# Running the first 128 tokens ahead of the second at the seams between stages of a decoder trunk

## The chip, the cores and the metric

The kernel runs on one core of one Trainium2 chip. The metric is the device time of one execution in microseconds, as the median over several runs. The engines are named as the profile names them: PE is TensorE's matrix multiplication and PEld its weight load, DVE is VectorE, ACT is ScalarE, POOL is GpSimd, SP is SyncE, whose queue issues the kernel's transfers. L12 is line 12 of the kernel that is spoken of; the changed kernel is longer, so the same helper has another line number there.

## The reference

Two layers of a decoder, 256 tokens of width 2048, in float32. Layer 0 mixes tokens with differential attention and an S5 state-space model side by side, layer 1 with RWKV-7. After each mixer comes a SwiGLU. Every mixer and every SwiGLU has an RMS norm ahead of it and one behind it.

```python
def _rwkv7_time_mix(x, mu, ...):
    x_prev = jnp.pad(x, ((0, 0), (1, 0), (0, 0)))[:, :-1]
    xx = x_prev - x
    xr, xw, xk, xv, xa, xg = (x + xx * mu[j] for j in range(6))
    r = xr @ w_r
    ...
    return out.astype(x.dtype) @ w_o

def _swiglu(h, w_gate, w_up, w_down):
    return (jax.nn.silu(h @ w_gate) * (h @ w_up)) @ w_down

for layer in range(DEPTH):
    gains = norm_gains[layer]
    h = _rmsnorm(x, gains[0])
    m = ...            # even: attention and S5, then w_out; odd: RWKV-7, then w_o
    x = x + _rmsnorm(m, gains[1])
    f = _swiglu(_rmsnorm(x, gains[2]), ffn_w_gate[layer], ffn_w_up[layer], ffn_w_down[layer])
    x = x + _rmsnorm(f, gains[3])
```

## The kernel before, in words

**Products.** The 256 tokens are two halves of 128, t = 0 and 1. A float32 product is made of three reduced-precision ones: each operand is split into a high and a low part, and the kernel adds high·high, high·low and low·high (`wmm`). The activations of one half are the stationary operand, 512 columns of the weights are moved through. One step of `wide` is one k (128 rows of the weights) for 512 columns, so three instructions of 128x512 for one half. Weights arrive in the order of use as chunks of eight 128x128 blocks (512 KB, two steps): a load on SP into `wr`, a cast on ACT into `wh`, a subtraction on DVE into `wl` (`chunk_load`, L321, L326, L327 before). Each of the three has three buffers, and the next load waits until a buffer is free.

**Seams.** A stage ends with its last group of 512 columns, for both halves. What follows needs the mean square of the whole row, so nothing of the next stage can start before. There are four such seams, named here after their place: A, from the output projection of layer 0 to the first SwiGLU's gate; B, from its down product to RWKV's `wr`; C, from RWKV's `wo` to the second SwiGLU's gate; D, from the last down product to the kernel's output. At each seam a half goes through an epilogue: `Out.add` adds a partial sum (A, C), sums the squares on ACT (L570) and multiplies by a gain (L571); L457 and L458 on DVE and L459 on POOL make the scale R. At A and C `stage` then adds the result to the residual (X, L1098, on DVE), multiplies by the next norm's gain row `gr` (L1099, on DVE for the first quad of four 128-column blocks, on POOL for the others), turns the blocks by "flips" on PE (L592, transposes into `pa`) and splits them into Z, high part on ACT (L403), low part on DVE (L409). At B the rows X are L1276, M = X·R1 is L1277, the flip goes into `pb`, ACT copies it to H (L1280), and `mix` makes x + xx·mu for 128 columns and all 256 tokens: L1249 on ACT, L1256 on DVE, the cast L403 into MX on ACT.

**Order.** A scheduler with priorities (`hi()`, XP) sets the order of each engine's queue when the kernel is built; while `strict` is set, PE keeps program order. An engine takes its queue in that order, also when a later instruction would be ready. At the end of a stage `late=LATE` makes the last four steps run for half 0 and then for half 1, and `warm` puts 20 products of no use (L309) behind the last one.

**Behind seam B.** `k_steps` runs seven 128-column products of `wr` (NR = 7) with the weights as the stationary operand and all 256 tokens moved through, k by k as the mixes of a quad come. Later in the layer `Q` blocks (QB) and state blocks (XI) go through DRAM (`dr`) and are loaded again by SP.

Of the kernel before, what the change touches and what calls it, by code (L numbers as in the profile page):

```python
# [18 lines left out]
P = 128  # L19
T = 256  # L20
# [33 lines left out]
LATE = 4  # L54
# [12 lines left out]
W1, W2, W3 = 20, 20, 20  # L67
# [144 lines left out]
class Prog:  # L212
# [104 lines left out]
    def chunk_load(self, c, raw=False, hp=None, pool=False):  # L317
        nc = self.nc
        with self.tc.high_priority(offset=HP if hp is None else hp):
            r = self.wp.tile([P, CB * P], F32, tag="wr", name=f"wr{c}")  # L320
            nc.sync.dma_start(r, self.d["wst"][c])  # L321
            if raw:
                return (r,)
            h = self.wp.tile([P, CB * P], F32R, tag="wh", name=f"wh{c}")
            l = self.wp.tile([P, CB * P], F32R, tag="wl", name=f"wl{c}")
            nc.scalar.copy(h, r)  # L326
            (nc.gpsimd if pool else nc.vector).tensor_tensor(l, r, h.bitcast(F32), op=ALU.subtract)  # L327
            return (h, l)

    def block(self, w, k, m, raw=False, pool=False):  # L330
# [4 lines left out]
        if b % CB == 0:  # L335
            c = b // CB
            self.wcur = self.ahead.pop(c, None) or self.chunk_load(c, raw, pool=pool)
# [4 lines left out]
    def blocks(self, w, k, m, n=4):  # L342
# [3 lines left out]
        for i in range(n):  # L346
            self.block(w, k, m + i)
# [173 lines left out]
    def wide(self, w, n, zH, zL, ks, pss, nb=4, late=0, hook=None, first=True, last=True):  # L521


        ks, held = list(ks), []
        o = [ps[:, :nb * P] for ps in pss]
        for a, k in enumerate(ks):
            self.lab(w)
            W = self.blocks(w, k, n, nb)
            f, e = first and a == 0, last and a == len(ks) - 1
            if a >= len(ks) - late:  # L530
                held.append((k, W, f, e))
                continue
            for t in range(2):
                self.wmm(o[t], zH[k], zL[k], W, t, f, e)
# [13 lines left out]
    class Out:  # L548


        def __init__(self, p, m, l, j, n=NW, xs=None):
            self.p, self.m, self.l, self.j, self.xs, self.i = p, m, l, j, xs, 0
            self.ss = [p.sp.tile([P, 3, n], F32, tag=f"ss{t}", name=p.nm("ss"), bufs=1) for t in range(2)]

        def add(self, pss, c, n=512, part=None, last=False):
            p, nc = self.p, self.p.nc
            v, gp = nc.vector, nc.gpsimd
            g, cs = p.gain_row(self.l, self.j, c, n), slice(c, c + n)
            for t in range(2):
                ss, m, ps = self.ss[t][:, :, self.i:self.i + 1], self.m[t][:, cs], pss[t][:, :n]  # L560
                junk = lambda: p.tmp("j", [P, n])
                xt = None
                if self.xs is not None:
                    xt = p.tmp("xt", [P, n])
                    nc.sync.dma_start(xt, self.xs[t][:, cs])
                with p.hi():
                    if part is not None:
                        v.tensor_tensor(m, ps, part[t][:, cs], op=ALU.add)
                        ps = m
                    nc.scalar.activation(junk(), ps, AF.Square, accum_out=ss[:, 0])  # L570
                    (gp if part is not None and not last else v).tensor_tensor(m, ps, g, op=ALU.mult)  # L571
                    if xt is not None:
                        (v if last else gp).tensor_tensor(xt, xt, m, op=ALU.mult)  # L573
                        nc.scalar.activation(junk(), m, AF.Square, accum_out=ss[:, 2])
                        nc.scalar.activation(junk(), xt, AF.Copy, scale=2.0, accum_out=ss[:, 1])
            self.i += 1
# [134 lines left out]
    def even(self):  # L711
        nc, v, gp = self.nc, self.nc.vector, self.nc.gpsimd
        with self.phase("ev"):
# [54 lines left out]
            def main():  # L768
# [41 lines left out]
                for n in range(NW):  # L810
                    pss = [self.pg(), self.pg()]
                    e = n == NW - 1
                    yield from self.wide("out", 4 * n, mH + gH, mL + gL, range(OH, 16), pss, late=LATE if e else 0)
                    out.add(pss, n * 512, part=part, last=e)
# [10 lines left out]
            self.warm(W1)  # L825
# [255 lines left out]
    def ffn(self, x, l, macc):  # L1081
# [4 lines left out]
        with self.phase(f"ffn{l}"):  # L1086
            sH, sL = ([self.slot("Z", 4, F32R) for _ in range(2)] for _ in range(2))
            zH, zL = ([s[k // 8][:, k % 8] for k in range(KD)] for s in (sH, sL))
            sx = [self.sp.tile([P, NW], F32, tag=f"sx{t}", name=self.nm("sx"), bufs=1) for t in range(2)]
# [19 lines left out]
            pss = [[self.pg(), self.pb()] for _ in range(3)]  # L1109
            grp = [(gw, 0), (uw, 0), (gw, 4)]  # L1110
            g = self.gain_row(l, 2, 0)
            for t in range(2):
                for k, n in ((0, 1), (1, 3)):
                    stage(t, k, n, g[:, k * P:(k + n) * P], v)
                if t == 0:
                    held = [self.blocks(gw, k, 0) for k in range(4)]
                for k in range(4):
                    self.lab(gw)
                    self.wmm(pss[0][t], zH[k], zL[k], held[k], t, k == 0, False)
            for q in range(4):  # L1120
# [681 lines left out]
```

## Time and profile before

| what | value |
|---|---|
| median of 3 runs | 2651.56 us (2647.16 to 2653.05) |
| the profiled execution | 2639.7 us, of which its span is 2637.9 us |
| PE busy | 2508.4 us (95%) |
| DVE busy | 1643.5 us (62%) |
| ACT busy | 1189.5 us (45%) |
| POOL busy | 444.8 us (17%) |
| mean granted clock | 0.972 |

The profiled execution is some 12 us below the median of the timed runs; sums made from its rows are set against its own time. A row of the timeline gives start, duration, engine, line, operation, output and inputs, and in brackets how long its engine was idle before it and what ended that. Busy shares are means over stages with different limits: what a seam costs is read at the seam.

### The profile page before, as it was taken

The page shows a single profiled execution, that of the slowest core. Times are in us where ns is not written, and L with a number is a line of the kernel's source. Part 1 is how long each engine was busy: PE and PEld are TensorE (multiplying, and loading weights), DVE is VectorE, ACT ScalarE, POOL GpSimd, SP SyncE. Part 2 cuts the span into 40 slices and gives each one's busy share as a digit, 9 for nine tenths or more (in the row PEclk, how much of TensorE's full clock was granted, in tenths as well). Part 3 has the DMA queues.
Part 4 walks back from the last instruction along what each step waited for, and adds up shares of the span by engine and source line. Part 5 has one row for each costly group of instructions (what it writes and reads, how often), then busy time and mean ns, then how long its engine had stood idle before and what let it go on. Part 6 is the DMA issues. An engine that isn't in the chain of part 4 may idle for free. (4 is left out here: it accounts for less than half of the span.)

```text
span 2637.9 us, 36715 instructions
## 1 busy us (share of the span) xinstructions
PE 2508.4 (95%) x13816; PEld 2097.0 (79%) x13816; DVE 1643.5 (62%) x2370; ACT 1189.5 (45%) x1752; POOL 444.8 (17%) x694
## 2 busy tenths in 40 slices
PE   7998899899999999997899898999799999999999
PEld 7775658688888888886899877788688888888887
DVE  7877876555555555445568987768655555554444
ACT  5332335444444444444666643343444444444443
POOL 4765731200000000000115540111300000000000
PEclk9998899999999999998999998999899999999999
DMA  6332335655555555665467677765655555555565
GB/s 217 116 108 66 103 112 194 210 186 186 190 190 191 186 192 189 208 224 199 144 200 241 201 215 206 193 192 184 205 187 187 191 191 190 190 187 192 196 195 192
DMA packets 222754, 484.51 MB, mean 184 GB/s; under 512 B 78832, under 2 KB 109808, under 8 KB 220784
## 3 DMA queue, kind: packets, MB, share of 16 engines
q1 hardware_dynamic: 222576, 482.17, 56.7%
q8 instruction: 108, 1.77, 0.3%
q14 instruction: 70, 0.57, 0.1%
HBM read 454.31 MB, written 27.79 MB: 183 GB/s over the span
## 5 line engine op out<-in xcount | busy, mean ns | idle before, releaser
L327 DVE TENSOR_TENSOR wl<-wr,wh 128x1024 fp32r<-128x1024 f32 x760 | 946.0, 1246 | 790.2 <-ACT wh L326 784.7
L326 ACT CAST wh<-wr 128x1024 fp32r<-128x1024 f32 x768 | 807.7, 1052 | 1039.7 <-PE pb L302 728.3
L302 PE MATMUL pg<-wh,Z 128*128 128x512 f32 x1664 | 636.8, 394 | 0.5 <-DVE Z L409 0.4
L302 PE MATMUL pb<-wh,Z 128*128 128x512 f32 x1408 | 547.2, 389 | 0.1
L302 PEld LDWEIGHTS pg<-wh,Z 128*128 128x128 f32 x1664 | 314.0, 189 | 71.2 <-issue 4.9
L302 PE MATMUL pg<-wl,Z 128*128 128x512 f32 x832 | 325.2, 391 | 0.0
L302 PEld LDWEIGHTS pb<-wh,Z 128*128 128x128 f32 x1408 | 264.2, 188 | 55.7 <-ACT Z L403 0.5
L302 PE MATMUL pb<-wl,Z 128*128 128x512 f32 x704 | 273.9, 389 | 0.0
L302 PE MATMUL pg<-wh,PP 128*128 128x512 f32 x576 | 223.3, 389 | 0.0
L302 PE MATMUL pb<-wh,PP 128*128 128x512 f32 x576 | 223.1, 389 | 0.0
L302 PE MATMUL pg<-MX,wh 128*128 128x256 f32 x896 | 175.3, 292 | 9.4 <-ACT MX L403 9.3
L302 PEld LDWEIGHTS pg<-wl,Z 128*128 128x128 f32 x832 | 157.4, 189 | 30.9
L302 PE MATMUL pg<-wh,MX 128*128 128x512 f32 x512 | 176.4, 409 | 0.3 <-ACT KR L1400 0.3
L302 PE MATMUL pg<-Z,wh 128*128 128x256 f32 x736 | 151.5, 306 | 16.2 <-ACT wh L326 10.5
L302 PEld LDWEIGHTS pb<-wl,Z 128*128 128x128 f32 x704 | 132.2, 188 | 27.5
L302 PEld LDWEIGHTS pg<-MX,wh 128*128 128x128 f32 x896 | 144.2, 196 | 10.7 <-ACT MX L403 9.9
L302 PEld LDWEIGHTS pg<-Z,wh 128*128 128x128 f32 x736 | 122.0, 205 | 36.4 <-issue 19.7
L302 PE MATMUL pg<-MX,wl 128*128 128x256 f32 x448 | 130.4, 294 | 3.9 <-DVE wl L327 3.9
L459 POOL TENSOR_TENSOR ts<-ts,mhalf 128x1 f32<-128x1 f32 x10 | 6.5, 653 | 752.4 <-DVE ts L458 752.4
L302 PEld LDWEIGHTS pg<-wh,PP 128*128 128x128 f32 x576 | 108.1, 188 | 22.5
L302 PEld LDWEIGHTS pb<-wh,PP 128*128 128x128 f32 x576 | 108.1, 188 | 22.5
L573 POOL TENSOR_TENSOR xt<-xt,M 128x512 f32<-128x512 f32 x6 | 7.8, 1300 | 666.0 <-DVE M L571 666.0
(402 smaller groups left out, 3758.2 us busy)
## 6 DMA issues: line engine op xcount, KB each, us to landing
wr<-wst SPq DMA_DIRECT2D x776, 512.0 KB, 3.4
dr<-H SPq DMA_DIRECT2D x16, 512.0 KB, 4.2
CH<-dr SPq DMA_DIRECT2D x16, 512.0 KB, 5.4
dr<-X SPq DMA_DIRECT2D x6, 1024.0 KB, 4.4
X<-dr SPq DMA_DIRECT2D x6, 1024.0 KB, 6.2
gr<-cr SPq DMA_DIRECT2D x16, 256.0 KB, 2.8
dr<-ak SPq DMA_DIRECT2D x16, 256.0 KB, 4.0
ln<-lnb SPq DMA_DIRECT2D x8, 512.0 KB, 5.0
```

Of the source, the lines that this page charges most:

```text
L302: self.pe(self.nc.tensor.matmul(out, lhsT, rhs, start=start, stop=stop))
L326: nc.scalar.copy(h, r)
L327: (nc.gpsimd if pool else nc.vector).tensor_tensor(l, r, h.bitcast(F32), op=ALU.subtract)
L459: self.nc.gpsimd.tensor_tensor(r, ms, self.mhalf[:, 0:1], op=ALU.pow)
L573: (v if last else gp).tensor_tensor(xt, xt, m, op=ALU.mult)
```

## The change

At each seam the last steps of the ending stage's last group and the first steps of the next are run for half 0 first, and for half 1 afterwards from weights that were kept. The kept chunks beyond the three buffers are put into memory that is not in use at that time ("homes": S, CH, Z, PA, PB, PC, MA). The numbers of steps are 8 (`LO0`) at A's end, 8 at C's, 12 (`LD`) at B's and D's, and 12 (`LO1`) of gate and 14 (`LW`) of `wr` for the stages that begin.

```diff
-LATE = 4
+LO0, LO1, LW, LD = 8, 12, 14, 12
-W1, W2, W3 = 20, 20, 20
...
+    def skew(self, w, zH, zL, steps, late, homes=(), pre=None, post=None):
+        held, homes = [], list(homes)
+        def piece(t, a, W):
+            k, n, o, f, e = steps[a]
+            if pre:
+                pre(t, a)
+            self.lab(w)
+            self.wmm(o[t], zH[k], zL[k], W, t, f, e)
+            if e and post:
+                post(t, n, o[t])
+        for a, (k, n, *_) in enumerate(steps):
+            keep = a >= len(steps) - late
+            home = homes.pop(0) if keep and homes and len(self.order) % CB == 0 else (None, False)
+            W = self.blocks(w, k, n, home=home[0], pool=home[1])
+            piece(0, a, W)
+            yield 2
+            if keep:
+                held.append((a, W))
+            else:
+                piece(1, a, W)
+                yield 2
+        for a, W in held:
+            piece(1, a, W)
+            yield 2
```

The gate's start, and one of the ends; `pre` puts the staging of a quad ahead of a step, `post` the epilogue of a half (`Out.half`, the old `Out.add` for one half) behind its last step. The 2 in `homes` sends that chunk's subtraction to POOL, in two pieces of 512 columns.

```diff
-            pss = [[self.pg(), self.pb()] for _ in range(3)]
-            grp = [(gw, 0), (uw, 0), (gw, 4)]
...
+            def pre(t, a):
+                if (t, a) == (0, 0):
+                    stage(0, 0, 1, gs[0][:, :P], v)
+                    stage(0, 1, 3, gs[0][:, P:], v)
+                    quad(0, 1)
+                elif (t, a) in ((0, 4), (0, 8)):
+                    quad(0, a // 4 + 1)
+                elif (t, a) == (0, 10):
+                    quad(1, 0, v)
+                elif (t, a) in ((1, 0), (1, 4), (1, 8)):
+                    quad(1, a // 4 + 1)
+            steps = [(k, 0, g, k == 0, False) for k in range(LO1)]
+            self.run(self.skew(gw, zH, zL, steps, LO1, [(("PC", 2), False), (("PC", 2), 2), (None, False), (None, 2), (pa, False),
+                                                        (pb, 2)], pre))
+            self.run(self.wide(gw, 0, zH, zL, range(LO1, KD), g, first=False))
+            self.run(self.wide(uw, 0, zH, zL, range(KD), u))
...
+            homes = [(("Z", 4), False)] * 3 if l else [(("PA", 4), False)] * 4
+            self.run(self.skew(dw, pH, pL, steps, LD, homes, post=lambda t, n, ps: out.half(t, NW - 1, ps, last=True)))
             x = self.load_x([a[:] for a in xs])
-            self.warm(W3 if l else W2)
```

The four gain rows are loaded together (`gs`, tiles e) with the priority XP; quad 1 of half 0 is turned ahead of the first gate product. In RWKV the first four `wr` columns become one group of 512 with the tokens as the stationary operand, whose result is turned back by eight flips (`turn`) and goes to DRAM in one tensor `r4`; columns 4 to 6 follow one after another. The mixes of a quad become 128x512 tiles: L1337 is ACT's scale of M, L1342 the copy to H, L1350 (L1347 for half 1) the product with mu on POOL, L1351 and L1352 DVE's product and sum, L418 the cast into MB on ACT. The mixes for the low-rank products, which are not part of `wr`, keep their form: L1300 and L1304 on ACT. The memory of the mixes (MX) is split in MA and MB, that of the SwiGLU's products (PP) in PA, PB and PC.

DVE's queue at seam A, from half 0's gain product on. Before (L571 gain product, L568 add, L1098 the rows X, L1099 the staging product; the two halves are M_4547 and M_4548):

```order
L571 TENSOR_TENSOR M_4547<-M_4547,t_4985 128x512
L457 TENSOR_REDUCE ts_5016<-ss_4549 128x1
L458 TENSOR_SCALAR ts_5017<-ts_5016 128x1
L327 TENSOR_TENSOR wl_5075<-wr_5072,wh_5074 128x1024
L568 TENSOR_TENSOR M_4548<-pg_4888,Z_3710 128x512
L1098 SCALAR_TENSOR_TENSOR X_5029<-M_4547,ts_5018,X_5029 128x128
...
L327 TENSOR_TENSOR wl_5134<-wr_5131,wh_5133 128x1024
L571 TENSOR_TENSOR M_4548<-M_4548,t_4985 128x512
...
L1098 SCALAR_TENSOR_TENSOR X_5030<-M_4548,ts_5024,X_5030 128x512 x3
L1099 TENSOR_TENSOR M_4547<-X_5029,gr_5048 128x128
```

And in the changed kernel (L613 gain product, L610 add, L1146 the rows X, L1147 the staging product):

```order
L613 TENSOR_TENSOR M_4547<-M_4547,t_4960 128x512
...
L1146 SCALAR_TENSOR_TENSOR X_5007<-M_4547,ts_4996,X_5007 128x512 x3
L342 TENSOR_TENSOR wl_5087<-wr_5084,wh_5086 128x1024
L610 TENSOR_TENSOR M_4548<-pg_4888,Z_3710 128x512
L613 TENSOR_TENSOR M_4548<-M_4548,t_4960 128x512
L472 TENSOR_REDUCE ts_5000<-ss_4550 128x1
L473 TENSOR_SCALAR ts_5001<-ts_5000 128x1
L1146 SCALAR_TENSOR_TENSOR X_5008<-M_4548,ts_5002,X_5008 128x512 x4
L342 TENSOR_TENSOR PC_5036<-wr_5034,PC_5036 128x1024
L1147 TENSOR_TENSOR M_4547<-X_5007,e_5015 128x128
L1147 TENSOR_TENSOR M_4547<-X_5007,e_5015 128x384
```

Half 0's X rows now stand ahead of half 1's add, but the first staging product of half 0 still stands behind half 1's X rows. POOL's queue at the same place, in the changed kernel (L474 is R's power; e_5017 is the gain row of quad 1):

```order
L474 TENSOR_TENSOR ts_5002<-ts_5001,mhalf 128x1
L342 TENSOR_TENSOR PC_5074<-wr_5072,PC_5074 128x512 x2
L342 TENSOR_TENSOR wl_5110<-wr_5107,wh_5109 128x512 x2
L1147 TENSOR_TENSOR M_4547<-X_5007,e_5017 128x512
L1147 TENSOR_TENSOR M_4548<-X_5008,e_5017 128x512
```

The two chunks' subtractions stand there between R and the first staging product; before, R was followed by L1099 at once. ACT's queue at seam B in the changed kernel, first at the first quads of half 0 and then at the last quads of half 1 (pb_10392 is the first quad's flip; MA_10869 to MA_10981 are the mixes for the low-rank products):

```order
L1337 ACTIVATE M_8639<-X_10333,ts_10342 128x512 x2
L612 ACTIVATE j_10325,ss_8642<-pb_9918 128x512
L1337 ACTIVATE M_8639<-X_10333,ts_10342 128x512
L616 ACTIVATE j_10329,ss_8642<-M_8640 128x512
L617 ACTIVATE j_10331,ss_8642<-xt_10323 128x512
L1342 COPY H_10374<-pb_10392 128x4x128
```

```order
L1300 ACTIVATE MA_10869<-H_10374,n_8635 128x255 x8
L1342 COPY H_10375<-pb_10568 128x4x128
L1342 COPY H_10375<-pb_10594 128x4x128
L1300 ACTIVATE MA_10870<-H_10375,n_8635 128x255 x3
L1304 ACTIVATE m_10909<-H_10375,n_8635 128x256
L1300 ACTIVATE MA_10870<-H_10375,n_8635 128x255
L1300 ACTIVATE MA_10981<-H_10374,n_8635 128x255 x4
...
L418 CAST MB_10378<-XI_10574 128x4x128
```

Before, the last quad of all 256 tokens stood in the same way behind such mixes:

```order
L1280 COPY H_10428<-pb_10888 128x4x128
L1249 ACTIVATE MX_11172<-H_10427,n_8663 128x255 x5
L326 CAST wh_10826<-wr_10824 128x1024
L1249 ACTIVATE MX_11172<-H_10427,n_8663 128x255 x2
L1249 ACTIVATE MX_11173<-H_10428,n_8663 128x255 x3
...
L403 CAST MX_10430<-m_10894 128x256
```

So half 1's squares and scales of half 0 stand ahead of the first copy to H, and low-rank mixes ahead of half 1's last casts. SP's queue in RWKV, where QB is first loaded, before and in the changed kernel:

```order
L1624 DMA CH_14752<-dr_11348 128x1024
L1631 DMA QB_14736<-dr_11348 64x4x64
L1632 DMA MV_14754<-dr_11352 64x4x64
L1448 DMA XI_14655<-dr_11353 64x32x32 x2
L1631 DMA QB_14736<-dr_11348 64x4x64
L1632 DMA MV_14754<-dr_11352 64x4x64
```

```order
L1733 DMA CH_14561<-dr_11157 128x1024
L1740 DMA QB_14545<-dr_11157 64x4x64
L1741 DMA MV_14563<-dr_11161 64x4x64
L1740 DMA QB_14545<-dr_11157 64x4x64
L1741 DMA MV_14563<-dr_11161 64x4x64
L1733 DMA CH_14704<-dr_11157 128x1024
L1550 DMA XI_14464<-dr_11162 64x32x32 x2
```

Both QB loads, which stood on either side of the XI loads, now stand ahead of them.

More of the change, by code (lines that the diff above doesn't have):

```diff
@@ L340, in block, with blocks @@
         return tuple(t[:, s] for t in self.wcur)
-    def blocks(self, w, k, m, n=4):
+    def blocks(self, w, k, m, n=4, pool=False, home=None):
         o = len(self.order) % CB * P
@@ L519, in wmm, with wide @@
         self.mm(ps, zl[:, ts], h, False, stop)
-    def wide(self, w, n, zH, zL, ks, pss, nb=4, late=0, hook=None, first=True, last=True):
-        ks, held = list(ks), []
+    def wide(self, w, n, zH, zL, ks, pss, nb=4, hook=None, first=True, last=True):
+        ks = list(ks)
         o = [ps[:, :nb * P] for ps in pss]
@@ L551, in __init__ @@
         def __init__(self, p, m, l, j, n=NW, xs=None):
-            self.p, self.m, self.l, self.j, self.xs, self.i = p, m, l, j, xs, 0
+            self.p, self.m, self.l, self.j, self.xs, self.g = p, m, l, j, xs, {}
             self.ss = [p.sp.tile([P, 3, n], F32, tag=f"ss{t}", name=p.nm("ss"), bufs=1) for t in range(2)]
-        def add(self, pss, c, n=512, part=None, last=False):
-            p, nc = self.p, self.p.nc
-            v, gp = nc.vector, nc.gpsimd
[L558 to L576, printed above, removed]
@@ L1275, in rwkv_keys @@
                 with self.hi():
-                    v.scalar_tensor_tensor(x[t][:, cs], m[t][:, cs], R0[t], x[t][:, cs], op0=ALU.mult, op1=ALU.add)
-                    v.tensor_scalar(m[t][:, cs], x[t][:, cs], R1[t], None, op0=ALU.mult)
-                    ps = self.pb()
-                    self.flip(ps, m[t][:, cs])
-                    nc.scalar.copy(self.half(hs, 4 * q, 4, t), ps.rearrange("p (a b) -> p a b", b=P))
-            for k in range(4 * q, 4 * q + 4):
-                with self.hi():
-                    mix(0, rr, k)
-                rs = next(steps)
+                    nc.scalar.copy(d, ps.rearrange("p (a b) -> p a b", b=P))
@@ new lines, in turn @@
+                nc.sync.dma_start(r4[:, :, t * P:(t + 1) * P], d)
+        self.strict = True
+        pss = [self.pg(), self.pg()]
+        self.run(self.skew("wr", *rr, [(k, 0, pss, k == 0, False) for k in range(LW)], LW, homes, pre))
+        self.run(self.wide("wr", 0, *rr, range(LW, KD), pss, first=False))
+        rt = [self.tmp("ak", [P, 512]) for _ in range(2)]
+        for t in range(2):
+            with self.hi():
+                nc.scalar.copy(rt[t], pss[t])
+        self.strict = False
@@ L1600, in wo @@
         zH, zL = ({g * GP + p: oT[g][:, a + p] for p in range(GP)} for a in (0, GP))
-        for n in range(NW):
+        ks = range(g * GP, g * GP + GP)
+        for n in range(NW - 2 if out else NW):
             pss, cs = [self.pg(), self.pg()], slice(n * 512, n * 512 + 512)
-            yield from self.wide("wo", 4 * n, zH, zL, range(g * GP, g * GP + GP), pss, late=LATE)
+            yield from self.wide("wo", 4 * n, zH, zL, ks, pss)
             if out:
-                out.add(pss, n * 512, part=part, last=n == NW - 1)
+                out.add(pss, n, part)
                 continue
```

208 lines of the change are left out of this document (139 added, 69 removed).

## The prediction

> **What bounds the kernel now.** I read the page's busy times first, then TensorE's waits, then the places that those waits name. TensorE is the bound:
>
> ```profile
> span 2637.9 us, 36715 instructions
> PE 2508.4 (95%) x13816; PEld 2097.0 (79%) x13816; DVE 1643.5 (62%) x2370; ACT 1189.5 (45%) x1752; POOL 444.8 (17%) x694
> ```
>
> Only 129.5 us of the span have TensorE idle, so the change can win that at most, or the part of it that lies where it works. TensorE's waits over the whole span (engine, line, what it waited for, us in total, times, longest):
>
> ```profile
> PE pa L592 <- DVE M L1099: 19.1, 2, 9.9
> ...
> PE pb L592 <- DVE M L1277: 11.5, 2, 7.0
> ```
>
> The first is the flips (transposes) of seams A and C, the second those of seam B. With seam B's two waits for ACT further down (2.70 and 6.57) the three seams hold 39.9 us of visible idle time. Two stretches by window (us, then busy of PE, PEld, DVE, ACT, POOL, the granted clock, DMA share, GB/s), seam A from its last product to the next stage's first, and the wr stage behind seam B:
>
> ```profile
> 484.10:497.10 13.00, 3.76 (x26) 2.59 (x25) 11.29 (x20) 7.07 (x19) 3.24 (x3) 0.78 0.73 268
> 1251.10:1305.00 53.90, 47.16 (x359) 46.54 (x360) 35.19 (x66) 39.66 (x85) 9.05 (x46) 0.89 0.40 125
> ```
>
> At the seam DVE is busy 11.29 of 13.00 us: the seam is a chain on DVE, and what matters is the order of DVE's queue.
>
> **Seams A and C.** Seam A in the timeline (start, us, operation, idle before it and what ended it), first TensorE, then DVE, then ACT's square:
>
> ```profile
> 483.92 0.39 PE L302 MATMUL pg<-wh,Z 128*128 128x512 f32 x1
> 484.15 2.36 PE L309 MATMUL pa<-cg 128*128 128x256 bf16 x20
> 495.68 1.34 PE L592 MATMUL pa<-cg,M 128*128 128x128 f32 x4 [9.17 <-DVE M L1099]
> 497.07 0.79 PE L302 MATMUL pg<-wh,Z 128*128 128x512 f32 x1
> ```
>
> ```profile
> 485.26 0.68 DVE L568 TENSOR_TENSOR M<-pg,Z 128x512 f32<-128x512 f32 x1
> 485.86 2.86 DVE L1098 SCALAR_TENSOR_TENSOR X<-M,ts,X 128x128 f32<-128x128 f32 x5
> 488.64 1.22 DVE L327 TENSOR_TENSOR wl<-wr,wh 128x1024 fp32r<-128x1024 f32 x1
> 489.77 0.69 DVE L571 TENSOR_TENSOR M<-M,t 128x512 f32<-128x512 f32 x1
> ...
> 491.39 2.87 DVE L1098 SCALAR_TENSOR_TENSOR X<-M,ts,X 128x128 f32<-128x128 f32 x5 [0.67 <-POOL ts L459]
> 495.24 2.51 DVE L1099 TENSOR_TENSOR M<-X,gr 128x128 f32<-128x128 f32 x4 [0.98 <-DMA gr<-cr]
> ```
>
> ```profile
> 485.98 0.63 ACT L570 ACTIVATE s<-M 128x512 f32<-128x512 f32 x1 [0.54 <-DVE M L568]
> 486.52 0.19 ACT L570 ACTIVATION_READ_ACCUMULATOR s<-M 128x1 f32 x1
> ```
>
> Call T1 the end of the last product, 483.92 + 0.39 = 484.31. Before, the first flip starts at T1 + 11.4 and the first gate product at T1 + 12.8. The 20 warm products lie inside that wait and end 9.17 us before the first flip, so taking them away is worth 0 (their cover is DVE's chain).
>
> The change lets half 0 end eight steps earlier. A step of one half is three 512-wide products; such products start about 0.23 apart (497.07 aside: 483.92 to 484.15), so T0 = T1 − 24 x 0.227 = T1 − 5.4. If half 0's staging followed half 0's own epilogue, its first flip would come near T0 + 7 and the seam would shrink by some 10 us. But DVE's rows (in the section on the change) have half 1's whole epilogue ahead of the first L1147 of half 0. So the sum over DVE's queue from T0 is: add 0.68, square 0.63 + 0.19, product 0.69, reduce, scale and POOL's power 0.93 (from 489.77 + 0.69 to 491.39), five X rows 2.86, one weight subtract 1.22: 7.2, with about 0.1 at each hand-over 8.0. Then the same for half 1: 0.68 + 0.82 + 0.69 + 0.93 + 2.87, then the PC subtract 1.22, then the 128-wide L1147 (the least of its kind below, 0.29): 7.5, with hand-overs 8.1. First flip at T0 + 16.1 = T1 + 10.7: 0.7 earlier than before, not 10. Bounds: if DVE stood idle at T1 it would be T1 + 8.1, a gain of 3.3.
>
> Then the first gate product. It now stands behind the flips of quads 0 and 1 of half 0, and quad 1's L1147 is POOL's, behind four subtract pieces of two weight chunks. The prices: ACT's cast from the page, the subtract on POOL, and the same product on both engines (min/median/max ns):
>
> ```profile
> L326 ACT CAST wh<-wr 128x1024 fp32r<-128x1024 f32 x768 | 807.7, 1052 | 1039.7 <-PE pb L302 728.3
> ```
>
> ```profile
> L327 POOL TENSOR_TENSOR wl<-wr,wh x8: 2402/2570/6188, 1382.8 to 1523.3; 128x1024 fp32r<-128x1024 f32 x8
> L1099 POOL TENSOR_TENSOR M<-X,gr x12: 1272/1290/1616, 496.0 to 1898.8; 128x512 f32<-128x512 f32 x12
> L1099 DVE TENSOR_TENSOR M<-X,gr x8: 293/552/1371, 495.2 to 1890.9; 128x128 f32<-128x128 f32 x4, 128x384 f32<-128x384 f32 x4
> ```
>
> A piece is half of 2.57, 1.3. The second chunk's cast is on ACT behind half 1's square (about T0 + 9.5) and three 1.05 casts and a square: T0 + 13.5; two pieces 2.6, L1147 1.3: T0 + 17.4; four flips 1.1: first product at T0 + 18.6 to 19.4, that is T1 + 13.2 to 14. So +0.4 to +1.2 against 12.8. Behind it half 0's steps use weights twice as fast (a 512 KB chunk per 1.36 us instead of 2.72), and PA's and PB's chunks are cast only after all that, so one more short wait: I take +1.5 in all. The four gain rows stand on SP behind the chunk whose buffer the first subtract frees at T0 + 8, and have eight us to land: 0. Before, the gr load ended a 0.98 us wait, which goes, but DVE's queue is late there in its stead.
>
> POOL beside DVE is not free here. The 384-wide L1099 on DVE takes 0.55, but 1.37 where POOL's L1099 ran beside it (POOL's first starts at 496.0, inside DVE's four from 495.24 to 497.75): +0.82 a collision. Before, POOL was idle while DVE made X; now it has four pieces there. None colliding gives 0, four give +3.3; I take one, +1.0, since the casts hold POOL's pieces back until half of the X rows are made. Seam A: +2.5 (range −3.3 + 1.5 = −2 to 1.5 + 3.3 + a second short wait of 1.2 = +6). Seam C has the same orders and the same wait ahead of its first flip, so +2.5 too:
>
> ```profile
> 1890.19 1.34 PE L592 MATMUL pa<-cg,M 128*128 128x128 f32 x4 [9.89 <-DVE M L1099]
> ```
>
> The Trainium skill, "SBUF — State Buffer", section "SBUF: two separate sides", says that DVE and GpSimd share one port pair as an exclusive lock and that an operation of DVE with two SBUF inputs blocks for the whole of a GpSimd operation that reads SBUF. The 1.37 us row agrees with it, and by that rule every piece would collide: it is the first rival below.
>
> **Seam B and the wr products.** TensorE there, then DVE and ACT:
>
> ```profile
> 1241.65 1.11 PE L592 MATMUL pb<-cg,M 128*128 128x128 f32 x4 [6.97 <-DVE M L1277]
> 1247.26 1.11 PE L592 MATMUL pb<-cg,M 128*128 128x128 f32 x4 [4.49 <-DVE M L1277]
> 1251.07 1.01 PE L302 MATMUL pg<-MX,wh 128*128 128x256 f32 x3 [2.70 <-ACT MX L403]
> ...
> 1293.59 1.01 PE L302 MATMUL pg<-MX,wh 128*128 128x256 f32 x3 [6.57 <-ACT MX L403]
> ```
>
> ```profile
> 1237.07 2.74 DVE L1276 SCALAR_TENSOR_TENSOR X<-M,ts,X 128x512 f32<-128x512 f32 x4 [0.36 <-POOL m L1250]
> ```
>
> ```profile
> 1248.41 0.58 ACT L1280 COPY H<-pb 128x512 f32<-128x512 f32 x1 [5.02 <-PE pb L592]
> 1249.03 1.70 ACT L1249 ACTIVATE m<-H,n 128x255 f32<-128x255 f32 x4
> ```
>
> Ahead of the first flips lie 6.97 idle and the 2.36 of warm products, so T1 is about 1232.4 and the first wr product comes 18.7 later. Now T0 = T1 − 12 x 0.68 = T1 − 8.2, and half 0's chain ends near T1 + 1: its two flips come at once. But then ACT's queue has half 1's squares ahead of the copies of half 0's H: two scales 0.63 each (as the square's main part), square 0.82, scale 0.63, two squares 0.82 each, two copies 0.58 each, so 5.5 us, to T1 + 6.9 (R and its scales start at T1 + 1.1; hand-overs 0.3). Then POOL's two products 1.3 each; DVE behind half 1's four X rows (2.74) and a weight subtract (1.22) adds them, and ACT casts: first product between T1 + 11.3 (no wait on DVE) and T1 + 13.3; I take 13.3, because the four X rows and the subtract stand ahead in DVE's queue: −5.4.
>
> Inside the products three waits take the place of the one of 6.57. Half 0's quads 2: POOL has four subtract pieces (5.2) and then 1.3, against some 9 us of products at the low clock, so about 4.9. Half 1's start: 2.4 (flip, copy, 1.3 on POOL, add, cast after the last product of half 0's stage). Half 1's quads 2: ACT has 8 L1300 ahead of the copy and 18 between copy and cast, at 1.70/4 = 0.42: 3.4 + 1.2 + 7.6 + 0.6 = 12.8, less four steps' products and flips 3.6: 9.2. Sum 16.5, +9.9. The product count: 192 of 256 columns at 0.119 (22.9; the window's 47.16/359 at clock 0.89 gives 0.117) become 96 of 512 at 0.227 (21.8), plus 8 flips of r, at most twice 1.11. That cancels to 0, and r4's transfers run under the products of columns 4 to 6. Each long wait is followed by a stretch at the lower clock (0.89 over this window against 1.00); three waits instead of one are worth +0.5. Seam B: −5.4 + 9.9 + 0.5 = +5 (range −2, with the first product at T1 + 11.3 and the 4.9 gone, to +10, with the port of the first rival).
>
> The Trainium skill, "TensorE: Matmul & The Clock Gate", section "HAM oscillation — how this bites in real kernels", has the clock fall after gaps over about 3.4 us. The 0.78 and 0.89 above agree; by it two of the three waits would cool the array, and at 3.4 us of half speed each (1.7 lost) B would come out up to 2.9 us above my +5.
>
> **The SP queue in rwkv.** SP issues and TensorE at the fourth wait:
>
> ```profile
> 1592.83 2.12 SPq L1448 DMA_DIRECT2D XI<-dr  x2
> 1594.99 1.65 SPq L1631 DMA_DIRECT2D QB<-dr  x1
> ```
>
> ```profile
> 1599.57 2.05 PE L302 MATMUL pa<-QB,CH 128*128 128x128 f32 x8 [6.82 <-DMA QB<-dr]
> ```
>
> The second QB load stands in SP's queue behind the XI loads, which wait for their data until 1592.83. In the changed order both QB loads stand ahead of them. Nothing else of that product is late then; it would go at once. Gain 0 to 6.8; I take 6, because only its own queue place is seen to hold it.
>
> **Seam D.** Half 1's last product waits on DVE for half 0's four L1769:
>
> ```profile
> 2625.73 0.39 PE L302 MATMUL pb<-wh,PP 128*128 128x512 f32 x1
> ```
>
> ```profile
> 2625.76 2.74 DVE L1769 SCALAR_TENSOR_TENSOR X<-M,ts,X 128x512 f32<-128x512 f32 x4 [0.65 <-POOL ts L459]
> 2628.41 0.68 DVE L571 TENSOR_TENSOR M<-pb,gr 128x512 f32<-128x512 f32 x1
> ```
>
> With half 0 done 8.2 us earlier, the L571 of half 1 starts behind its square, at 2626.12 + 0.82 = 2626.9: −1.5, and the chain behind it is unchanged (−2 to 0).
>
> **Sum.** 2.5 + 2.5 + 5 − 6 − 1.5 = +2.5. The profiled execution took 2639.7 (span 2637.9 and 1.8 around it), 11.9 below the median of the runs; the difference is carried over to the median: 2651.56 + 2.5 = 2654.
>
> **Rivals.** (1) The port: all pieces collide. At A and C four pieces x 0.82 = 3.3 instead of 1.0, at B two L1350 and six pieces (4.9): +2.3 + 2.3 + 4.9 on top, 2663.6. For it: the 1.37 row. Against: the pieces may fall into DVE's waits. It decides where half 1's X rows at the seam average over 1.1 instead of 0.72. (2) Faster: seams A, B, C come out level, since half 1's epilogue is short and POOL's pieces come early, and only SP's and D's gains stay: 2651.56 − 6.8 − 1.5 = 2643. For it: A's bound of −3.3 and the −5.4 ahead of B's first product; it decides where B's three waits stay under 12. (3) The halves truly overlap, A and C shrink by 8 each: 2654 − 5 − 16 = 2633. Against: DVE's queue order is fixed. (4) The QB wait stays because something else is late: 2654 + 6 = 2660.
>
> **How the numbers follow.** Chances: forecast 0.45, (1) 0.22, (2) 0.20, (3) 0.05, (4) 0.08. About 0.2% (5.3 us) is what a measurement of this kernel can tell from no change. The forecast's own range is 2648 to 2660: 0.30 within, 0.13 slower, 0.02 faster. (1) is slower; (2) faster but for 0.02; (3) faster; (4) 0.05 slower, 0.03 within. So faster 0.25, same 0.35, slower 0.40. The range 2639 to 2667 leaves out (3) and the outer ends of (1) and (2).
>
> **What would show it.** Right: at A and C the first flip 10 to 12 us after the last product, released by DVE L1147; POOL's L342 pieces ahead of quad 1; at B a wait of 8 us or more for ACT L418 in half 1; no QB wait. Wrong: first flips of A within 5 us of the last product, or B's waits under 12 in sum, or X rows of half 1 over 1.1.

## The result: slower, and the profile after

The changed kernel takes 2665.23 us (median, 2662.11 to 2669.99), the kernel before 2649.36 beside it (2642.96 to 2653.05): ratio 1.0063, interval 1.0044 to 1.0083, so slower by 0.4 to 0.8%. The forecast was 2654, range 2639 to 2667.

The page's head after, and TensorE's waits over the span:

```profile
span 2660.3 us, 36318 instructions
PE 2500.7 (94%) x13648; PEld 2081.1 (78%) x13648; DVE 1652.0 (62%) x2340; ACT 1187.5 (45%) x1733; POOL 489.2 (18%) x708
```

```profile
PE pa L633 <- DVE M L1147: 31.6, 4, 15.4
PE pg L301 <- ACT MB L418: 28.9, 4, 13.3
...
PE pa L301 <- DMA QB<-dr: 3.3, 1, 3.3
...
PE pb L301 <- DMA QB<-dr: 2.5, 1, 2.5
```

TensorE is busy 8 us less and idle 30 us more. The flips' wait of seams A and C grew from 19.1 to 31.6, and the waits for ACT's cast of the mixes, 9.3 before (into MX), are 28.9 (into MB). Seam A (TensorE, DVE, POOL):

```profile
501.03 0.45 PE L633 MATMUL pa<-cg,M 128*128 128x128 f32 x1 [14.12 <-DVE M L1147]
...
505.44 4.04 PE L301 MATMUL pg<-PC,Z 128*128 128x512 f32 x12
```

```profile
491.65 5.77 DVE L1146 SCALAR_TENSOR_TENSOR X<-M,ts,X 128x512 f32<-128x512 f32 x4 [0.67 <-POOL ts L474]
497.34 2.28 DVE L342 TENSOR_TENSOR PC<-wr,PC 128x1024 fp32r<-128x1024 f32 x1
499.54 4.55 DVE L1147 TENSOR_TENSOR M<-X,e 128x128 f32<-128x128 f32 x3
```

```profile
492.01 3.19 POOL L342 TENSOR_TENSOR PC<-wr,PC 128x512 fp32r<-128x512 f32 x2 [0.39 <-ACT PC L338]
495.16 3.38 POOL L342 TENSOR_TENSOR wl<-wr,wh 128x512 fp32r<-128x512 f32 x2
498.50 9.20 POOL L1147 TENSOR_TENSOR M<-X,e 128x512 f32<-128x512 f32 x6
```

T1 is 486.91 here. The first flip comes at T1 + 14.1 (before 11.4), the first gate product at T1 + 18.5 (12.8). Half 1's four X rows take 1.44 each in the mean, the PC subtract 2.28 where it took 1.2, while POOL runs. The first row, which began 0.36 ahead of POOL's first piece, ended as early as if alone; each of the other three took 1.0 more. The second of them:

```profile
492.32 1.75 DVE L1146 SCALAR_TENSOR_TENSOR X<-M,ts,X 128x512 f32<-128x512 f32 x1
```

Seam B:

```profile
1240.28 1.09 PE L633 MATMUL pb<-cg,M 128*128 128x128 f32 x8 [0.39 <-DVE M L1335]
1254.71 0.79 PE L301 MATMUL pg<-wh,MB 128*128 128x512 f32 x1 [13.34 <-ACT MB L418]
...
1270.31 3.17 PE L301 MATMUL pg<-MA,MB 128*128 128x512 f32 x6 [5.09 <-ACT MB L418]
...
1298.39 1.22 PE L301 MATMUL pg<-MA,MB 128*128 128x512 f32 x2 [8.37 <-ACT MB L418]
1301.59 2.07 PE L301 MATMUL pg<-MA,MB 128*128 128x512 f32 x4 [1.97 <-DVE MB L424]
...
1344.09 13.65 PE L301 MATMUL pg<-MA,wr 128*128 128x256 f32 x62 [1.24 <-POOL MA L1305]
```

The last row, 62 low-rank products that begin behind a wait of 1.24 on POOL, is in every version and serves as a landmark. The window from the first `wr` product to it (columns as before), before and after:

```profile
1251.10:1320.80 69.70, 61.74 (x426) 59.06 (x426) 38.45 (x74) 46.42 (x103) 10.45 (x64) 0.92 0.44 138
```

```profile
1254.70:1344.10 89.40, 68.86 (x339) 57.56 (x339) 44.64 (x64) 43.83 (x86) 24.66 (x74) 0.83 0.40 123
```

At seam D the last gain product comes 1.5 earlier against T1 = 2649.77, as forecast:

```profile
2650.59 0.69 DVE L613 TENSOR_TENSOR M<-pb,gr 128x512 f32<-128x512 f32 x1 [3.89 <-ACT j L612]
```

Cut at the last products (T1 of each seam) and at the landmark, the profiled executions of the kernels that follow compare like this (us):

| stretch | before | after | nopool | b_undone | seams_first | fold_first | b_eight |
|---|---|---|---|---|---|---|---|
| start to T1 of A | 484.3 | 486.9 | 488.5 | 486.9 | 485.6 | 488.2 | 488.8 |
| A: to T1 of B | 748.2 | 753.0 | 752.1 | 751.8 | 747.4 | 746.7 | 753.8 |
| of it, to the first gate product | 12.8 | 18.5 | 14.1 | 18.5 | 10.1 | 3.1 | 18.5 |
| B: T1 to the landmark | 88.4 | 104.2 | 101.4 | 88.2 | 88.7 | 89.0 | 87.7 |
| RWKV: landmark to T1 of C | 557.3 | 550.0 | 556.8 | 552.7 | 545.8 | 543.9 | 557.7 |
| C: to T1 of D | 748.0 | 755.7 | 753.8 | 754.6 | 750.0 | 750.4 | 754.9 |
| D: T1 to the end | 11.8 | 10.5 | 10.1 | 10.0 | 11.0 | 11.5 | 10.5 |

After less before: A +4.8, B +15.8, RWKV −7.3, C +7.7, D −1.3, and +2.6 ahead of A, 22.4 in all. The 2.6 isn't the change's: two kernels that are the kernel before as far as A reach T1 at 488.7 and 490.4. Nor are 22.4 the medians' 15.9: the profiled execution before was a quick one. Each column is one execution, and stretches of the same code differ: four builds with the changed seam A (after, b_undone, b_cover, b_eight) take 751.8 to 754.0 over A and 754.6 to 755.7 over C; two with the old one (before, qb_act) take 748.2 and 748.3 over A, 748.0 and 749.3 over C.

### The profile page after: what moved, and what is told of

Read it like the earlier page. It is cut to its first block, busy times and chain, and to the rows that moved or that the text cites. A ratio compares the mean times of both kernels' runs of the same rounds, so it can differ in the third digit from the quotient of the medians.

```text
span 2660.3 us, 36318 instructions
## 1 busy us (share of the span) xinstructions
PE 2500.7 (94%) x13648; PEld 2081.1 (78%) x13648; DVE 1652.0 (62%) x2340; ACT 1187.5 (45%) x1733; POOL 489.2 (18%) x708
## 5 line engine op out<-in xcount | busy, mean ns | idle before, releaser
L342 DVE TENSOR_TENSOR wl<-wr,wh 128x1024 fp32r<-128x1024 f32 x736 | 916.5, 1246 | 771.5 <-ACT wh L338 770.9
L338 ACT CAST wh<-wr 128x1024 fp32r<-128x1024 f32 x747 | 785.7, 1053 | 1030.4 <-PE pb L301 699.3
L474 POOL TENSOR_TENSOR ts<-ts,mhalf 128x1 f32<-128x1 f32 x10 | 8.4, 839 | 749.3 <-DVE ts L473 749.3
L301 PE MATMUL pg<-wh,MB 128*128 128x512 f32 x288 | 102.6, 418 | 17.5 <-ACT MB L418 15.5
L301 PE MATMUL pg<-Z,wl 128*128 128x256 f32 x368 | 107.4, 296 | 3.0 <-DVE wl L342 3.0
L301 PE MATMUL pg<-MA,wh 128*128 128x256 f32 x512 | 101.1, 291 | 0.3 <-ACT wh L338 0.3
L301 PE MATMUL pg<-wh,PA 128*128 128x512 f32 x256 | 99.8, 390 | 0.0
L301 PE MATMUL pb<-wh,PA 128*128 128x512 f32 x256 | 99.6, 389 | 0.0
L301 PE MATMUL pg<-wh,MA 128*128 128x512 f32 x236 | 81.8, 407 | 2.2 <-DVE X L1714 2.2
L301 PEld LDWEIGHTS pg<-MA,wh 128*128 128x128 f32 x512 | 81.5, 193 | 0.7 <-ACT wh L338 0.5
L301 PEld LDWEIGHTS pg<-wh,MB 128*128 128x128 f32 x288 | 56.4, 197 | 31.1 <-ACT MB L418 15.9
```

What stands on the lines that cost most here:

```text
L301: self.pe(self.nc.tensor.matmul(out, lhsT, rhs, start=start, stop=stop))
L342: (nc.gpsimd if pool else nc.vector).tensor_tensor(l[:, cs], r[:, cs], h[:, cs].bitcast(F32), op=ALU.subtract)
L474: self.nc.gpsimd.tensor_tensor(r, ms, self.mhalf[:, 0:1], op=ALU.pow)
```

## Experiments

Each ratio below is to the kernel before as it ran beside that kernel: 2649.21 us for nopool, alldve, b_undone and fill, 2645.79 for before_fill, b_cover, qb_act and seams_first, 2645.99 for b_eight and fold_first.

### Is it POOL's pieces? (nopool, alldve)

nopool: the changed kernel with all weight subtractions on DVE (every 2 in `homes` becomes False). alldve: the quads' staging products of A and C on DVE too.

```diff
...
-(("PC", 2), 2), (None, False), (None, 2), (pa, False), (pb, 2)
+(("PC", 2), False), (None, False), (None, False), (pa, False), (pb, False)
...
```

> The changed kernel with every weight subtraction that it had given to POOL put back on DVE (12 pieces at seams A and C, 8 at B); nothing else is edited, and the staging products of the later quads stay on POOL. Port theory (a POOL operation that reads SBUF holds up a DVE operation with two SBUF inputs): the pieces are gone, but POOL's staging products now start right behind R and meet half 1's X rows, so these stay near 1.4 us each at A and C; the first gate product still comes sooner, because quad 1's product is no longer behind four pieces: 18.5 after the last product at A falls to 14 or 15. At B the four X rows fall from 5.6 to about 4. Together about -11, 2654 us. Rival (the long X rows are DMA traffic or something else, and POOL only relieved DVE): DVE gets ten more subtractions of 1.22, of which one or two stand ahead at each seam: +5, 2670 us.

> As the run without POOL pieces, and the staging products of all quads of the two SwiGLUs are on DVE too, so that POOL has no long operation at seams A and C. Port theory: half 1's four X rows there fall from 5.77 to 2.9, the PC subtraction from 2.28 to 1.22, and the first gate product comes about 12.5 after the last product instead of 18.5, although DVE has six products of 0.69 more: -6 at A, -6 at C, about -4 at B: 2649 us. Rival (DVE is simply overloaded at the seam, the slow rows come from elsewhere): X rows stay at 1.4, six products and two subtractions more stand in DVE's queue: +3 at each of A and C, 2672 us.

nopool: 2660.34, ratio to before 1.0050 (1.0033 to 1.0067). alldve: 2664.24, 1.0062 (1.0044 to 1.0080). Seam A in nopool (T1 488.46), DVE and then TensorE:

```profile
493.20 2.74 DVE L1146 SCALAR_TENSOR_TENSOR X<-M,ts,X 128x512 f32<-128x512 f32 x4 [0.67 <-POOL ts L474]
```

```profile
498.56 1.27 PE L633 MATMUL pa<-cg,M 128*128 128x128 f32 x4 [10.10 <-DVE M L1147]
```

```profile
501.79 1.12 PE L633 MATMUL pa<-cg,M 128*128 128x128 f32 x4 [1.96 <-POOL M L1147]
...
513.77 1.20 PE L301 MATMUL pg<-PA,Z 128*128 128x512 f32 x4 [2.37 <-DVE Z L424]
```

```profile
496.50 5.23 POOL L1147 TENSOR_TENSOR M<-X,e 128x512 f32<-128x512 f32 x1 [3.34 <-DMA e<-cr]
```

The X rows are back at 2.74 (they were expected to stay near 1.4 each), so POOL's pieces had lengthened them. The first gate product comes at T1 + 14.1 instead of 18.5; at C 15.4 instead of 19.8. But little of these 4.4 us each is kept: POOL's first product now takes 5.23, where it took 1.3, beside subtractions and products of DVE that keep their length; half 0 waits 2.37 for Z later on; and half 1's first product stands at T1 + 28.5 instead of 29.6. The stretches A, B and C fall by 0.9, 2.8 and 1.9, 5.6 in all, and the first of them is inside the spread of the same code. RWKV's stretch is 6.8 longer in this execution; the second QB load stands behind the XI loads again and its wait is back (6.5, below). The median fell by 4.9, not by the 11 expected, and its interval overlaps that of the changed kernel.

alldve missed its 2649 by 15. The second quad's flips wait there for DVE, whose queue has all six products ahead of Z (4.71 at 505.85), and the first gate product comes at T1 + 16.9 and 18.1. The times don't tell nopool and alldve apart.

### Is it seam B? (b_undone)

The changed kernel with `rwkv_keys` as before (seven columns k by k, all 256 tokens, memory MX), and `late=4` at the end of layer 0's down product.

> The changed kernel with seam B as before: the down product of layer 0 ends with four late steps, and wr runs k by k over seven columns with all 256 tokens from 128-column mixes; A, C and D stay changed. By the sum over stages seam B costs 15.8 of the 22.4 us between the two profiles: 2665 - 16 = 2649 us, 2656 if the 7 us that the values stage gained belong to seam B's changed order and go back with it. Rival (B's waits only stand where later waits would stand anyway): -5 or less, 2660 us or more.

2653.54, ratio 1.0018 (1.0005 to 1.0032): 11.7 of the change's 15.9 are seam B, between the two cases expected. The stage takes 88.2 as before, the others stay within 3 us.

### Is it the clock? (fill, before_fill)

fill: dummy products in the changed kernel's waits (112 at A and C; 100, 40, 14 and 62 ahead of half 0's first and third and half 1's first and third quad at B). before_fill: the kernel before with more of its own.

```diff
-W1, W2, W3 = 20, 20, 20
+W1, W2, W3, W4 = 92, 72, 0, 96   # at A, B, the end, C
```

> The changed kernel with TensorE's waits filled by products of no use, as the old warm loops but longer: 112 at A and C, and in wr 100 ahead of the first product, 40 ahead of step 8 of half 0, 14 and 62 ahead of steps 0 and 8 of half 1; each ends ahead of what TensorE waits for. Clock theory (the waits cost more than their length, since the granted clock is 0.5 for 3 to 17 us behind them): the waits stay as long, but the products behind them run at full pace: -7 at B, -1.5 at A and C each, 2655 us. Rival (the products behind a wait are held by DVE and ACT anyway, so their pace is free): 0 to -3, 2662 to 2665 us.

> The kernel before with 92 dummy products at seam A, 72 at B and 96 at C instead of 20 each, none at the end. Clock theory (time at the low clock behind the waits is lost time): with the clock at full in the stretches behind the seams some 6 us are won, 2643. Rival (products at the low clock run while the next staging rows are made, so they cost little): within 1.5 of 2649.3, with longer waits in their place.

fill: 2668.42, 1.0072 (1.0049 to 1.0095), above both cases; B falls by 1.4 with the clock at 0.92 instead of 0.83. before_fill: 2648.53, 1.0007 (0.9995 to 1.0018). Seam A in before_fill, in the wait, at its end and behind it (same columns), and behind it in the kernel before:

```profile
490.40:500.50 10.10, 10.07 (x93) 8.78 (x90) 9.25 (x16) 4.46 (x10) 2.03 (x2) 1.00 0.64 228
500.50:503.20 2.70, 0.85 (x5) 0.48 (x5) 1.89 (x4) 2.61 (x10) 1.08 (x1) 1.00 1.07 427
503.20:507.00 3.80, 3.38 (x8) 2.42 (x9) 2.02 (x9) 0.91 (x3) 3.17 (x5) 0.62 0.72 236
```

```profile
497.10:501.00 3.90, 3.90 (x9) 2.63 (x10) 2.06 (x9) 0.90 (x3) 3.25 (x5) 0.50 0.73 235
```

The wait is filled, yet the clock falls behind it (0.62, and 0.50 without the filling), and in 3.8 us TensorE gets eight instructions done, nine before. At A and B the stretches are as long as before to 0.2 us; C's is 2.7 longer. (The total alone would not decide: in this build both QB loads stand ahead of XI, which was worth some 5 us in qb_act, below.) So warming buys nothing here, and where it did raise the clock (B in fill) the staging waits took most of it back: the clock theory falls, with 1.4 us at B as the most that it was worth.

### Where B's 15.8 us come from (b_cover, b_eight)

In both, columns 4 to 6 are made k by k, not behind all of columns 0 to 3. b_cover keeps the skew of 14 steps and puts them between half 1's pieces. b_eight runs only eight steps ahead, and the staging of the half quads is put in another order to fit:

```diff
-        self.run(self.skew("wr", *rr, [(k, 0, pss, k == 0, False) for k in range(LW)], LW, homes, pre))
-        self.run(self.wide("wr", 0, *rr, range(LW, KD), pss, first=False))
+        self.run(self.skew("wr", *rr, [(k, 0, pss, k == 0, False) for k in range(8)], 8, homes[1:5], pre))
+        quad(0, 3)
+        cols(range(0, 4))
+        quad(1, 3)
+        cols(range(4, 8))
+        self.run(self.wide("wr", 0, *rr, range(8, 12), pss, first=False, last=False))
+        cols(range(8, 12))
+        self.run(self.wide("wr", 0, *rr, range(12, KD), pss, first=False))
+        cols(range(12, KD))
```

> The changed kernel with one difference at seam B: the products of r's columns 4 to 6 are not all behind columns 0 to 3, but stand between half 1's pieces, 36 of them behind each of half 1's first three quads. Theory (the waits of half 1 come from work that used to cover them having been moved behind): the waits of 8.4 and 2.0 at half 1's third and fourth quads go, and B's stage falls by 6 to 10: 2655 to 2659. Rival (the chain over ACT, POOL and DVE sets the end of this stage whatever TensorE does in it): the waits shrink but the stage does not, within 3 of 2665.

> The changed kernel with one difference at seam B: half 0 runs only the first 8 steps of columns 0 to 3 ahead; behind half 1's eight follow columns 4 to 6 of those steps, and then the other eight steps with both halves together, each four with columns 4 to 6 behind them. Theory (the staging of the eight half quads ends some 61 us after the last product, before and after the change alike, 1293.59 - 1232.48 and 1301.59 - 1239.90; what the change costs at B is the 15 us more of products that stand behind the last of it, 26.9 against 11.6): with 10 us of products behind the last staging B's stage is within 3 of before, so the time is 12 to 15 below the changed kernel's 2665: 2650 to 2653. Rival (the finer staging and the low clock cost it): the stage falls by less than 6, 2659 or more.

b_cover: 2670.96, 1.0095 (1.0071 to 1.0119), outside both cases; B is no shorter. The staging waits of half 1's later quads are gone, and the columns wait for their own weights instead, 8.1 in six waits. The code has the kept chunks hold two of the three buffers then, which is the likely reason. The longest:

```profile
1305.28 0.51 PE L301 MATMUL pa<-MB,wh 128*128 128x256 f32 x2 [2.94 <-ACT wh L338]
```

b_eight: 2657.01, 1.0034 (1.0020 to 1.0047). B takes 87.7, as before the change, although the first product still waits 17.01 and every mix is still made by halves:

```profile
1261.05 5.36 PE L301 MATMUL pg<-MA,MB 128*128 128x512 f32 x12 [17.01 <-ACT MB L418]
...
1330.31 13.65 PE L301 MATMUL pg<-MA,wr 128*128 128x256 f32 x62 [1.24 <-POOL MA L1305]
```

The last low part of `wr`'s mixes, on DVE before the change, after it and in b_eight:

```profile
1294.41 1.42 DVE L409 TENSOR_TENSOR MX<-m,MX 128x256 fp32r<-128x256 f32 x4
```

```profile
1300.85 1.28 DVE L424 TENSOR_TENSOR MB<-XI,MB 128x512 fp32r<-128x512 f32 x2
```

```profile
1302.59 0.68 DVE L424 TENSOR_TENSOR MB<-XI,MB 128x512 fp32r<-128x512 f32 x1
```

It ends 63.4, 62.2 and 60.7 us after T1, though the first `wr` product came at T1 + 18.6, 14.8 and 18.5: in these three the chain over DVE, ACT and POOL sets that, not TensorE's start. What counts is how much product work is left then. The low-rank products that follow `wr` start here, before and after:

```profile
1305.17 14.41 PE L302 MATMUL pg<-MX,wr 128*128 128x256 f32 x66
```

```profile
1328.44 14.41 PE L301 MATMUL pg<-MA,wr 128*128 128x256 f32 x66
```

From the last wait on the mixes it was 11.6 us to them (1293.59 to 1305.17) and is 26.9 (1301.59 to 1328.44): columns 4 to 6, which lay under the staging, had been moved behind it. Counted from the end of the last low part, it is 9.3 before, 26.3 after and 10.5 in b_eight. In b_cover that part itself ends later, 68.9 us after T1, and 19.4 are left behind it, so its stage is as long as the changed kernel's. The total is above the 2650 to 2653 expected, with the QB wait of 6.7 back in this build.

### The QB wait (qb_act)

The kernel before with the second half of the first QB load issued from ACT's queue.

> The kernel before with one edit: the second half of the first QB load is issued from ACT's queue, so that it no longer stands behind the XI loads on SP's. Theory (its queue place alone holds it): the wait of 6.8 on QB falls under 3 and the time falls by 3 to 6, 2643.5 to 2646.5. Rival (something else is late, the prediction's rival 4): a wait of about the same length stays under another name and the time stays within 1 of 2649.3.

2640.74, ratio 0.9976 (0.9964 to 0.9989); beside it the kernel before took 2645.79, and the wait is 1.8. SP's queue in the changed kernel, and in nopool, whose code here is the same:

```profile
1609.72 0.89 SPq L1740 DMA_DIRECT2D QB<-dr  x1
...
1611.37 0.61 SPq L1740 DMA_DIRECT2D QB<-dr  x1
...
1617.04 4.48 SPq L1550 DMA_DIRECT2D XI<-dr  x2
```

```profile
1617.64 1.93 SPq L1550 DMA_DIRECT2D XI<-dr  x2
1619.61 1.46 SPq L1740 DMA_DIRECT2D QB<-dr  x1
```

```profile
1624.06 2.05 PE L301 MATMUL pa<-QB,CH 128*128 128x128 f32 x8 [6.49 <-DMA QB<-dr]
```

With the second load ahead of XI the wait is 3.3 in the changed kernel, 3.4 in b_cover, 2.3 in before_fill, and 1.7 and 1.2 in the next two kernels; behind it, it is 6.5 to 6.8. The place is a by-product of the scheduler's plan: edits elsewhere turned it over from build to build.

The place does not by itself set the length of RWKV's stretch. That stretch in the kernel before, the changed kernel, b_cover and seams_first (columns as above):

```profile
1320.83:1878.10 557.27, 517.79 (x4200) 460.11 (x4201) 432.92 (x744) 274.20 (x502) 156.77 (x179) 0.95 0.69 202
1344.09:1894.07 549.98, 512.10 (x4198) 453.54 (x4198) 429.76 (x747) 273.37 (x501) 158.35 (x180) 0.97 0.71 206
1345.87:1904.28 558.41, 523.73 (x4198) 462.97 (x4198) 431.27 (x747) 273.49 (x501) 155.91 (x180) 0.94 0.69 203
1321.60:1867.40 545.80, 511.52 (x4198) 454.09 (x4198) 430.63 (x747) 273.28 (x501) 159.75 (x180) 0.97 0.71 208
```

The last three have both loads ahead of XI, and so has before_fill, with 558.8. TensorE is busy up to 12 us longer for as many products where the granted clock is lower. What sets the clock over this stretch is open.

### Half 0 first in DVE's queue (seams_first, fold_first)

b_undone with two edits: the subtractions of A and C on DVE as in nopool, and DVE's queue pinned there: half 0's two L1147 ahead of the PC subtracts, half 1's X row of a quad behind half 0's Z of that quad (`mark[q]` is half 0's last subtraction of quad q).

```diff
...
+                    with self.tc.issue_after(mark[q]):
+                        stage(t, 4 * q, 4, gs[q], eng)
```

fold_first puts the gain into the split besides (`split(..., self.gain(l, 2, k + i))` for each 128 columns), so there is no L1147 and no gain row to load.

> Seam B is as before; A, C and D are as changed, with two differences: at A and C all weight subtractions are on DVE, and DVE's queue is made to take half 0's two products with the gain row straight behind half 1's epilogue, ahead of the PC subtracts and of half 1's X rows; half 1's X row of a quad follows half 0's last subtraction of that quad. Theory (the order of DVE's queue keeps the halves from overlapping): the first flip comes 5 to 6 us after the last product instead of 14 to 15, the first gate product after 9.5 to 11 instead of 18.5 (before: 12.8 and 13.1), so each of A and C falls by 8 against the changed kernel and the time is near 2653.5 - 16 = 2637.5. Rival (the work has only moved): half 1's staging is then late, TensorE waits 4 us or more for half 1's first rows, and of the 16 at most half stays: 2645 to 2650.

> As the run before with half 0 first in DVE's queue and seam B as before (2632.3), with one more difference: the gain row is not multiplied ahead of the flips but put into the split behind them, one block of 128 at a time, so that neither the gain rows' loads nor those products stand between half 0's X rows and its flips. Theory (of the 10.1 us between the last product and the first gate product 3.3 to 3.5 are the wait for the gain rows): the flips start within 1 us of the last product, the first gate product 5 to 7 us behind it, and the time falls by 3 to 5 at each of A and C: 2622 to 2626. Rival (32 more small operations each on ACT and DVE per seam take it back: at 0.28 against 0.68 for four, some 3.5 us of DVE a seam): the first product comes early but half 1's rows late, within 3 of 2632.

seams_first: 2632.32, ratio 0.9958 (0.9934 to 0.9982). fold_first: 2631.78, 0.9938 (0.9916 to 0.9959). Both beat both kernels; fold_first, for which 2622 to 2626 was expected, came as its rival had it. Seam A in seams_first (T1 485.59; DVE, then TensorE):

```profile
491.84 0.76 DVE L1154 TENSOR_TENSOR M<-X,e 128x128 f32<-128x128 f32 x2 [3.32 <-DMA e<-cr]
```

```profile
492.28 1.28 PE L640 MATMUL pa<-cg,M 128*128 128x128 f32 x4 [6.70 <-DVE M L1154]
...
495.68 1.63 PE L301 MATMUL pg<-PC,Z 128*128 128x512 f32 x3
...
509.34 0.71 PE L301 MATMUL pb<-PC,Z 128*128 128x512 f32 x2
```

And in fold_first (T1 488.23), where the flips follow the last product at once:

```profile
488.07 1.03 PE L632 MATMUL pa<-cg,X 128*128 128x128 f32 x8
491.31 0.79 PE L301 MATMUL pg<-PC,Z 128*128 128x512 f32 x1 [2.21 <-ACT Z L419]
...
512.28 3.02 PE L301 MATMUL pb<-PC,Z 128*128 128x512 f32 x12
```

So the queue's order was a part of what kept the halves apart: with the subtractions on DVE the first gate product of A comes at T1 + 14.1 (nopool), with the order pinned as well at 10.1. Against b_undone the two edits take 4.5 off A and 4.6 off C, not the 8 expected of each. Starting earlier is not ending earlier: fold_first has the first gate product at T1 + 3.1, 7 us sooner than seams_first, but half 1's first product (pb) stands at T1 + 23.8 and T1 + 24.0 in the two. Between the two products DVE is busy all of the 13.7 us in seams_first and 16.1 of 21.0 us in fold_first, where TensorE is granted 0.67 of its clock. Against the kernel before, the seams themselves are about level (A −0.8 and −1.5, C +2.0 and +2.4, or +0.7 and +1.2 against qb_act). Most of the gain is RWKV's stretch, 11.5 and 13.3 shorter. The QB wait is 5.1 of that in seams_first and 4.0 in fold_first, which has a second one of 1.6; most of the rest is TensorE busy 6.3 and 5.7 less at clock 0.97, and whether the pinned order brings that is not shown.

## Why the prediction was right, and where it was not

The sign and the range held; the likeliest case did not come in. The first rival's mark, half 1's X rows over 1.1, was crossed (1.44), and its time, 2663.6, is 1.6 off, but that nearness is luck. It put 9.5 us on top for collisions with POOL; without POOL's pieces (nopool) A, B and C fall by 5.6. Its 4.9 at B is also six collisions at 0.82, where it names eight.

- **The frame of A and C was right.** DVE's queue, with half 1's epilogue ahead of half 0's staging, made the seam longer, not 10 us shorter, and pinning the queue the other way brought the first gate product to T1 + 10.1.
- **A and C, +2.5 each, measured +4.8 and +7.7.** The step that failed first is "I take one" collision "since the casts hold POOL's pieces back until half of the X rows are made". The first piece began at 492.01, 0.36 behind the X rows. Three of the four rows, the PC subtract and the first L1147s were slowed, at 1.0 a row. Without the pieces the first gate product is at T1 + 14.1, where the forecast without collisions was 13.2 to 14. But the stretches are then still 3.9 and 5.8 longer than before, so the second step that failed is "+1.5 in all" for the first gate product and what stands behind it: in nopool the later wait for Z alone is 2.37. The Trainium skill, "SBUF — State Buffer", section "SBUF: two separate sides", has DVE and GpSimd exclude each other at a shared port; the trace agrees: behind the first row, a row and a piece begin in turn, a pair every 1.7 us (0.7 and 1.3 alone, so the lock is nearly but not quite whole here), and in nopool it was POOL's product that was held up, at 5.23 for 1.3. The price of a collision had also been misread. The 1.37 row is a 128-wide L1099, whose like takes 0.29 alone, so it gave 1.08, not 0.82:

```profile
496.38 1.37 DVE L1099 TENSOR_TENSOR M<-X,gr 128x128 f32<-128x128 f32 x1
```

- **B, +5, measured +15.8.** First product at T1 + 14.8 (forecast 13.3; 13.4 in nopool): −3.8 for −5.4. The waits inside were well sized: 5.1 (4.9), 3.3 (2.4) and 10.3 (9.2), and 0.5 besides, 19.3 against 16.5. The term that failed is the low clock, "worth +0.5": for the same work (61.74 x 0.92 = 56.8 and 68.86 x 0.83 = 57.2) TensorE was busy 7.1 longer. But fill shows that this is not a price of its own: with the clock held up more of the time, the waits took most of it back. The sum of waits was the wrong way to count; b_eight shows the better one, the products left behind the last staging, 15.3 more. "That cancels to 0" was true of the amount of products and missed their place.
- **The QB wait, −6; the stretch measured −7.3, and that the two are close is luck.** The step "it would go at once" failed: with both loads ahead of XI 3.3 of the 6.8 stayed, and a second QB wait of 2.5 came behind it, so the waits on QB fell by 1.0. The rest of the −7.3 is mostly TensorE busy 5.7 less, at clock 0.97 instead of 0.95. b_cover has the same code and the same queue places there and takes 558.4, more than before. qb_act confirms that the place matters: 1.8 of the wait is left, and the time is some 5 lower. Not settled is what gives the clock; b_undone's stretch is 4.6 shorter than before with the wait still at 6.7, and there too TensorE is busy 5.4 less, at 0.96.
- **D, −1.5, measured −1.3.**
- **The other rivals.** Level seams (2) needed B's waits under 12. True overlap (3) is nearest to fold_first: the flips came right behind the last product, and the gain was not 8 a seam, since half 1's first product came no sooner than in seams_first. (4) is what nopool and b_eight met, in another build.

## What to carry to other kernels

Count a chain of staging by what stands behind its end, not by the waits inside: work moved from under a chain to behind it cost its whole length at B, whatever was gained at the head. A stage that started earlier gained only as far as the other half came earlier too. An edit that is planned by a scheduler also moves instructions elsewhere; look at the places of the loads that TensorE waits for before giving the edit the credit, and at another build with the same places before giving it to them.

## What the hardware showed that was not expected

- DVE's loss beside POOL is not a matter of single collisions: four two-input rows of 512 columns took 2.74 alone and 5.77 beside POOL's subtractions, three products 1.35 and 4.55 beside its products. The loss can fall on POOL as well: its product took 1.3 alone and 5.23 in nopool.
- The clock fell behind a wait that was filled: in before_fill no gap of TensorE at seam A was longer than 1.27 us, and from the last dummy product (490.25 + 10.22 = 500.47) to the first product (503.17) there are 2.7 us with the gaps and the flips in them; the next 3.8 us were granted 0.62. The Trainium skill, "TensorE: Matmul & The Clock Gate", section "HAM oscillation — how this bites in real kernels", has it that gaps over about 3.4 us cool the array; these 2.7 are less, even with the flips counted as a gap.
- The same code took 484.3 to 490.4 us to reach seam A, which is more than most terms of the sum: stretches have to be compared one by one.
